# Four-branch mixer layers: the attention part rebuilt around four query tiles, one score tile and gates as filler

## Chip, cores and metric

One core of a Trainium2 chip. The metric is the device time of one launch in microseconds; the median of three runs stands for the kernel.

## Reference

Two layers over 256 context and 1024 latent tokens of width 1024. One input projection feeds four token mixers of width 256: A neighbourhood attention (clamped 8 x 16 window with a learned bias), B latent attention with a shared rotary key, C a bidirectional linear recurrence, D grouped-query attention. Each mixer's output is multiplied by the silu of a gate path; the branches are projected, gated and summed:

```
x = layer_norm(x) * (1 + scale) + shift
p = x @ w_in                                # mixers, silu gates z, merge gates m
y[i] = attend(q, k, v) or recurrence        # 4 heads of 64, softmax over context + latent keys
out = sum(sigmoid(m[i]) * ((y[i] * silu(z[i])) @ w_branch[i]) for i in range(4)) @ w_out
x = layer_norm(alpha * x + gate * out) * ln_g + ln_b
```

Context queries see context keys only, and the last layer needs no context output. All is float32.

## The kernel before

Tokens lie in 10 tiles of 128 (2 of context, 8 latent), all shared storage in 12 slots of 128 x 1280 (`slot`). A float32 operand is split into two parts, so each product is three matmuls (`mm_a` L271 to L273, `mm_b` L279 to L281; `hi_lo` L284, L285; `split_w` L233, L234; weights come by `load_w` L248). A scheduler turns the program into one instruction order per engine: a step that stands earlier in the program gets an engine first, a waiting instruction holds those behind it. Every load and store is issued by the sync engine's (SP) queue.

Each layer runs g_proj; then a weave of (m_proj, a_proj) with (lru, g_att), in proportion to expected numbers of steps; m_att; a_att; merge; last; outp. `g_att`, `m_att` and `a_att` loop over 4 heads. A head loads keys (high rows over low rows, `load_k` L641) and values (`load_v` L646), then `attend` takes two query tiles at a time: `load_q` (L632; L634 for the rotary rows of m) into one of two tiles, the scores of both, then puts off the value product of that unit by one unit (`defer`). A dense score tile (`dense_scores`, L618) goes bank by bank, 512 + 512 + 256 columns in three rotating banks, each read by VectorE with scale and maximum (L620); `softmax` joins the maxima (L587), takes the exponential on ScalarE (L592), the reciprocal of the sum (L596) and multiplies the row by it, on VectorE for the first tile (L599), on ScalarE for the second (L601). In `a_att` the bias rows be and bm are loaded (L804, L805), scaled on GpSimd, and added to the window's scores (L839 to L854). `values` transposes two key blocks of two query tiles into one bank (L552), splits it, and multiplies (L568, L569). `put_u` computes the silu gate of 128 output channels, multiplies, and writes u to memory.

While m_att and a_att run, `tick` emits steps of `gates`, which computes the merge gates of branch 0 (the one merged last) and writes them to memory (L885, L886). `merge` then takes branches 2, 3 and 1 (gates on PE, sigmoid L928, product and sum L934, L935), `last` takes branch 0 with the gates read back. The weave around the change:

```
weave(("", chain((f"m_proj{l}", m_steps()), (f"a_proj{l}", a_steps())), W_A),
      ("", chain((f"lru{l}", lru_steps()), (f"g_att{l}", g_att())), W_B + 4 * len(dense_units())))
```

## Time and profile before

| | us |
|---|---|
| median of 3 runs (lowest, highest) | 3183.25 (3182.18, 3184.07) |
| profiled execution, its own span | 3176.4 |
| PE busy | 2806.6 (88%) |
| VectorE busy | 1659.0 (52%) |
| ScalarE busy | 1382.4 (44%) |
| GpSimd busy | 208.7 (7%) |

The span runs from the first to the last instruction; the time around it is what a run has more. PE's mean granted clock is 0.946 of full speed. In the first layer, projections and lru end and g_att begins at about 300, m_att runs from 548 to 840, a_att to 1091, merge and last to 1570; the second layer's attention ends at 2709. A name such as `m_att__q` is a tile with the stage that was current when it was made. Busy time of PE at the lower clock counts in full, so a busy PE can still be slow.

### The profile page before, as it was taken

What the parts mean: (1) busy time and instruction counts of PE and PEld (TensorE: products, weight loads), DVE (VectorE), ACT (ScalarE), POOL (GpSimd) and SP (SyncE); (2) the same over time, 40 slices, a digit from 0 to 9 for tenths busy, and PEclk for the clock granted to TensorE, in tenths of its full rate; (3) what the DMA queues carried; (4) which work ended last, traced back from release to release, by engine and by line L of the source; (5) the groups of instructions that cost most, each with busy time, mean ns of one, the idle gap of its engine ahead of it and who ended that gap; (6) DMA issues with size and microseconds to landing.
All of it is one profiled execution on the core that took longest, in us unless ns stands there. A gap on an engine that the chain in (4) does not pass through costs nothing.

```text
span 3176.4 us, 40938 instructions
## 1 busy us (share of the span) xinstructions
PE 2806.6 (88%) x14798; PEld 2317.9 (73%) x14798; DVE 1659.0 (52%) x4049; ACT 1382.4 (44%) x2546; POOL 208.7 (7%) x273
## 2 busy tenths in 40 slices
PE   7999978778878999999999899878777688999998
PEld 4787767666767877777768787667666576888877
DVE  5666655555555512232377656556566456223356
ACT  4366655545555512121234456555555455222230
POOL 1200000000000000000042210000000100000031
PEclk9999989888988999999999999999898889999999
DMA  7233222211233322222353323222212222222142
GB/s 264 80 105 117 63 77 80 77 61 64 65 101 95 92 68 65 63 77 62 99 185 101 117 76 116 84 70 74 77 56 72 86 76 90 77 60 60 54 149 84
DMA packets 304563, 281.01 MB, mean 88 GB/s; under 512 B 23400, under 2 KB 249960, under 8 KB 304360
## 3 DMA queue, kind: packets, MB, share of 16 engines
q1 hardware_dynamic: 304360, 278.40, 28.4%
q8 instruction: 116, 1.90, 0.2%
q14 instruction: 87, 0.71, 0.1%
HBM read 207.67 MB, written 70.66 MB: 88 GB/s over the span
## 4 chain that ended last, share of the span: by engine, by line
PE 63%; DMA 17%; DVE 5%; ACT 4%; SPq 3%; issue 2%; POOL 2%; DVEq 0%; POOLq 0%; ACTq 0%
PE merge__mm L279 6%; PE merge__mm L280 6%; PE merge__mm L281 6%; PE m_att__s L618 3%; DMA m_att__q<-start__qkm 2%; PE a_att__mm L279 2%; PE a_att__mm L280 2%; PE a_att__mm L281 2%; DMA m_att__ks<-outp__qkm 2%; SPq L632 2%; PE m_att__t L552 2%; PE a_att__t L552 2%; PE merge__s L279 2%; PE merge__s L280 2%; PE merge__s L281 2%
## 5 line engine op out<-in xcount | busy, mean ns | idle before, releaser
L279 PE MATMUL merge__mm<-xh,merge__whi 128*128 128x512 f32 (+1 forms) x960 | 360.3, 375 | 0.0
L281 PE MATMUL merge__mm<-xh,merge__wlo 128*128 128x512 f32 (+1 forms) x960 | 354.8, 370 | 0.0
L280 PE MATMUL merge__mm<-xl,merge__whi 128*128 128x512 f32 (+1 forms) x960 | 354.8, 370 | 0.0
L279 PEld LDWEIGHTS merge__mm<-xh,merge__whi 128*128 128x128 f32 x960 | 181.5, 189 | 63.1 <-issue 21.6
L618 PE MATMUL m_att__s<-m_att__ks,m_att__q 128*128 128x512 f32 (+1 forms) x400 | 126.7, 387 | 96.9 <-DMA m_att__ks<-outp__qkm 47.4
L233 ACT CAST merge__whi<-merge__wraw 128x512 fp32r<-128x512 f32 x144 | 79.1, 551 | 290.4 <-PE merge__mm L280 243.9
L281 PEld LDWEIGHTS merge__mm<-xh,merge__wlo 128*128 128x128 f32 x960 | 181.6, 189 | 30.7
L280 PEld LDWEIGHTS merge__mm<-xl,merge__whi 128*128 128x128 f32 x960 | 181.7, 189 | 28.9
L928 ACT ACTIVATE merge__tmp<-merge__mm 128x512 f32<-128x512 f32 (+1 forms) x120 | 66.4, 553 | 312.0 <-PE merge__mm L281 311.2
L234 DVE TENSOR_TENSOR merge__wlo<-merge__wraw,merge__whi 128x512 fp32r<-128x512 f32 x144 | 86.4, 601 | 193.3 <-ACT merge__whi L233 187.9
L620 DVE TENSOR_SCALAR_CACHE_REDUCE m_att__p<-m_att__s 128x512 f32<-128x512 f32 (+1 forms) x200 | 113.7, 588 | 115.3 <-PE m_att__s L618 114.3
L284 ACT CAST m_att__ph<-m_att__t 128x512 fp32r<-128x512 f32 x164 | 94.5, 584 | 171.7 <-PE m_att__t L552 126.3
L934 DVE TENSOR_TENSOR merge__tmp<-merge__s,merge__tmp 128x512 f32<-128x512 f32 (+1 forms) x80 | 51.1, 638 | 220.6 <-PE merge__s L281 220.6
L618 PEld LDWEIGHTS m_att__s<-m_att__ks,m_att__q 128*128 128x128 f32 x400 | 76.3, 206 | 112.3 <-DMA m_att__ks<-outp__qkm 42.2
L285 DVE TENSOR_TENSOR g_att__pl<-g_att__t,g_att__ph 128x512 fp32r<-128x512 f32 x154 | 104.7, 688 | 84.8 <-ACT g_att__ph L284 70.9
L618 PE MATMUL g_att__s<-g_att__ks,g_att__q 128*128 128x512 f32 (+1 forms) x400 | 110.0, 381 | 38.6 <-DMA g_att__ks<-outp__qkg 19.6
L285 DVE TENSOR_TENSOR m_att__pl<-m_att__t,m_att__ph 128x512 fp32r<-128x512 f32 x164 | 111.1, 687 | 55.6 <-ACT m_att__ph L284 54.9
L620 DVE TENSOR_SCALAR_CACHE_REDUCE g_att__p<-g_att__s 128x512 f32<-128x512 f32 (+1 forms) x200 | 112.0, 586 | 42.2 <-PE g_att__s L618 41.3
L284 ACT CAST g_att__ph<-g_att__t 128x512 fp32r<-128x512 f32 x154 | 88.1, 583 | 100.6 <-PE g_att__t L552 52.4
L568 PE MATMUL g_att__pv<-g_att__ph,g_att__vs 128*128 128x256 f32 x308 | 98.1, 326 | 30.6 <-ACT g_att__ph L284 29.9
L279 PE MATMUL a_att__mm<-xh,a_att__whi 128*128 128x512 f32 (+1 forms) x304 | 119.0, 391 | 1.6 <-ACT a_att__tmp L885 1.6
L962 POOL TENSOR_TENSOR merge__acc<-merge__acc,last__spare 128x512 f32<-128x512 f32 (+1 forms) x40 | 55.9, 1421 | 939.0 <-DVE last__spare L961 938.8
(425 smaller groups left out, 7870.4 us busy)
## 6 DMA issues: line engine op xcount, KB each, us to landing
merge__wraw<-in_w_in_dram SPq DMA_DIRECT2D x96, 256.0 KB
mod__wm<-in_w_mod_dram SPq DMA_DIRECT2D x48, 256.0 KB
g_proj__wm<-in_w_mod_dram SPq DMA_DIRECT2D x16, 512.0 KB
a_att__wraw<-in_w_in_dram SPq DMA_DIRECT2D x32, 256.0 KB
last__wraw<-in_w_out_dram SPq DMA_DIRECT2D x32, 256.0 KB
merge__wraw<-in_w_branch_dram SPq DMA_DIRECT2D x48, 128.0 KB
g_att__q<-start__qkg SPq DMA_DIRECT2D x40, 128.0 KB
m_att__q<-start__qkm SPq DMA_DIRECT2D x40, 128.0 KB
```

The lines of the kernel that those rows point to most:

```text
L233: act.copy(hi[:, :n], raw[:, :n])
L234: dve.tensor_sub(lo[:, :n], raw[:, :n], hi[:, :n])
L279: pe.matmul(ps, wh, xh, start=first and k == 0, stop=False)
L280: pe.matmul(ps, wh, xl, start=False, stop=False)
L281: pe.matmul(ps, wl, xh, start=False, stop=last and k == nk - 1)
L284: act.copy(hi, src)
L285: dve.tensor_sub(lo, src, hi)
L552: pe.transpose(tb[:n, c:c + 128], pts[qi][:, col:col + n], ident)
L568: pe.matmul(pv[:, :nq], vt[:n, vb, :], ph[:n, w], start=first, stop=False)
L618: pe.matmul(s[:, :w], qs[:, j, qi * 128:(qi + 1) * 128], k[:, c0:c0 + w], start=j == 0, stop=j == len(ks) - 1)
L620: dve.tensor_scalar(pt[:, c0:c0 + w], s[:, :w], scale, None, ALU.mult, ALU.max, accum_out=mx[:, ns:ns + 1])
L928: act.activation(sgm[:, :g[1]], pm[:, :g[1]], AF.Sigmoid)
```

## The change

Twelve slots become thirteen. Attention works on units of four query tiles, with query loads and value products of 512 columns. The three score banks become one tile, `wide`, and the dense reduction is a single instruction of 1280 columns that gives the negated scores and the bias of the exponential. Rows of P stay unnormalised: the sums go to a column of `rcp`, and `put_u` multiplies the output by their reciprocals (GpSimd spreads them, PE transposes them). Silu uses tanh. `values` and `put_u` are generators in a queue; `pump` emits a share of the waiting steps behind each score tile. A list of 12 jobs covers the heads of g, m and a, and each head's keys and values are asked for when the head before it starts. Gates of two branches, 1 and 0, are computed as filler at one rate over all of the attention, and merge reads those of branch 1 from memory. Lru is woven with the projections, g_att no longer is. The core of the diff (removed lines only where they are short; where a whole function is replaced, the lines printed above give way):

```diff
-RATE_A = 3.0
+G_PRE = 2
...
-    sl = ctx.enter_context(tc.tile_pool(name="sl", bufs=12))
+    sl = ctx.enter_context(tc.tile_pool(name="sl", bufs=13))
...
-    ps_s = ctx.enter_context(tc.tile_pool(name="ps_s", bufs=3, space=PSUM))
+    ps_s = ctx.enter_context(tc.tile_pool(name="ps_s", bufs=1, space=PSUM))
...
     def sbank():
-        return ps_s.tile([128, 512], F32, tag="s", name=nm("s"))
+        turns[1] = (turns[1] + 1) % 3
+        return wide[:, 512 * turns[1]:512 * turns[1] + 512]
...
+    wide = ps_s.tile([128, 1536], F32, name="wide")
...
-        gate_d = dram([KC, 128, NT], F32, "gates")
+        gate_d = {i: dram([KC, 128, NT], F32, f"gates{i}") for i in M_ORDER[4 - G_PRE:]}
...
+        def put_u(i, c, y, rcp=None):
             w = load_chunk(w_in, C_Z + 256 * i + 128 * c)
+            if rcp is not None:
+                dve.reciprocal(rcp[:, :, q0t:], rcp[:, :, q0t:])
             for g in qgroups:
                 gs = slice(g[0], g[0] + g[1])
                 ps = mm()
-                mm_b(ps[:, :g[1]], w, xs_g(g))
+                xs = xs_g(g)
+                for k in range(0, KC, 2):
+                    mm_b(ps[:, :g[1]], w[k:k + 2], lambda j: xs(k + j), k == 0, k == KC - 2)
+                    if k < KC - 2:
+                        yield
                 s = tmp()
-                act.activation(s[:, :g[1]], ps[:, :g[1]], AF.Sigmoid)
-                dve.tensor_mul(s[:, :g[1]], ps[:, :g[1]], s[:, :g[1]])
-                dve.tensor_mul(y[:, gs], y[:, gs], s[:, :g[1]])
+                act.activation(s[:, :g[1]], ps[:, :g[1]], AF.Tanh, scale=0.5)
+                dve.scalar_tensor_tensor(s[:, :g[1]], s[:, :g[1]], 1.0, ps[:, :g[1]], ALU.add, ALU.mult)
+                if rcp is not None:
+                    tb = tbank()
+                    r = tmp()
+                    t0, n = g[0] // 128, g[1] // 128
+                    for j in range(n):
+                        pool.tensor_copy(r[:, j * 128:(j + 1) * 128].rearrange("p (h e) -> p h e", h=2),
+                                         rcp[:, :, t0 + j:t0 + j + 1].to_broadcast([128, 2, 64]))
+                    for j in range(n):
+                        pe.transpose(tb[:, j * 128:(j + 1) * 128], r[:, j * 128:(j + 1) * 128], ident)
+                    dve.tensor_mul(y[:, gs], y[:, gs], tb[:, :g[1]])
+                dve.scalar_tensor_tensor(y[:, gs], y[:, gs], 0.5, s[:, :g[1]], ALU.mult, ALU.mult)
+                yield
             sp.dma_start(u_d[i][c, :, QS], y[:, QS])
+            yield
+        PUT = 4 * len(qgroups) + 1
...
+                yield from put_u(2, c, hs[0])
...
+        queue, later = [], []
...
+        def pump(shares):
+            for _ in range(-(-sum(q[1] for q in queue) // shares)):
+                if queue:
+                    step()
...
+        def attend(h, y, rcp, units, loadq, scores, vt):
             o = 64 * (h % 2)
             for qts, blocks in units:
                 qs = loadq(qts[0] * 128, 128 * len(qts))
                 pts = []
                 for qi, qt in enumerate(qts):
+                    pts.append(scores(qs, qt, qi, rcp[:, h % 2, qt:qt + 1]))
                     tick()
+                    pump(len(qts) - qi)
+                    yield
+                queue.append([values(o, y, qts, blocks, pts, vt), len(blocks) + 1])
...
         def values(o, y, qts, blocks, pts, vt):
             nq = 128 * len(qts)
+            pv = ps_v.tile([128, 512], F32, tag="pv", name=nm("pv"))
             nb = len(blocks)
+            def turn(vb, q0, cols):
                 tb = tbank()
+                w = 128 * len(cols)
+                for i, col in enumerate(cols):
+                    pe.transpose(tb[:, i * 128:(i + 1) * 128], pts[q0 + i][:, col:col + 128], ident)
                 ph = tp.tile([128, 512], F32R, tag="ph", name=nm("ph"), bufs=2)
                 pl = tp.tile([128, 512], F32R, tag="pl", name=nm("pl"), bufs=2)
+                hi_lo(ph[:, :w], pl[:, :w], tb[:, :w])
+                return vb, slice(128 * q0, 128 * q0 + w), ph[:, :w], pl[:, :w]
+            def product(i, vb, qr, ph, pl):
+                pe.matmul(pv[:, qr], vt[:, vb, :], ph, start=i == 0, stop=False)
+                pe.matmul(pv[:, qr], vt[:, vb, :], pl, start=False, stop=i == nb - 1)
             st = None
+            for i, b in enumerate(blocks):
+                nx = turn(*b)
                 tick()
                 if st:
+                    product(i - 1, *st)
                 st = nx
+                yield
+            product(nb - 1, *st)
             lo = tmp()
             act.copy(lo[o:o + 64, :nq], pv[64 - o:128 - o, :nq])
             t0 = qts[0] * 128
             dve.tensor_add(y[o:o + 64, t0:t0 + nq], pv[o:o + 64, :nq], lo[o:o + 64, :nq])
+            yield
+        def softmax(pt, nb, spans, scale, total):
+            if len(spans) == 1:
+                (c0, c1), = spans
+                act.activation(pt[:, c0:c1], pt[:, c0:c1], AF.Exp, bias=nb, scale=scale, accum_out=total)
+                return
             sums = small(2, "sums")
             for j, (c0, c1) in enumerate(spans):
                 act.activation(pt[:, c0:c1], pt[:, c0:c1], AF.Exp, bias=nb, scale=scale, accum_out=sums[:, j:j + 1])
+            dve.tensor_add(total, sums[:, 0:1], sums[:, 1:2])
+        def new_y():
+            return slot(s="y"), lc.tile([128, 2, TT], F32, tag="rcp", name=nm("rcp"), bufs=3)
         def dense_units():
+            u = [((0, 1), [(b, 0, [b * 128] * 2) for b in range(CT)])] if need_ctx else []
+            full = [(b, 0, [b * 128] * 4) for b in range(TT)]
+            return u + [(tuple(range(CT + 4 * j, CT + 4 * j + 4)), full) for j in range(2)]
         def dense_scores(ks, scale):
+            def f(qs, qt, qi, total):
                 nk = CTX if qt < CT else NT
                 pt = slot(s="p")
+                nb = small(1, "nb")
                 for c0 in range(0, nk, 512):
                     w = min(512, nk - c0)
                     for j, k in enumerate(ks):
+                        pe.matmul(wide[:, c0:c0 + w], qs[:, j, qi * 128:(qi + 1) * 128], k[:, c0:c0 + w],
                                   start=j == 0, stop=j == len(ks) - 1)
+                dve.tensor_scalar(pt[:, :nk], wide[:, :nk], -scale, None, ALU.mult, ALU.min, accum_out=nb)
+                softmax(pt, nb, [(0, nk)], -1.0, total)
                 return pt
             return f
...
-            t = tp.tile([128, 3, 256], F32R, tag="q", name=nm("q"), bufs=2)
+            t = tp.tile([128, 3 if rope else 2, 512], F32R, tag="q", name=nm("q"), bufs=2)
...
+        def g_job(h):
+            def load():
                 if h % 2 == 0:
+                    g_kv[h // 2] = load_k(qk_g, 2, 64 * (h // 2)), load_v(v_g, h // 2)
+                return g_kv[h // 2]
+            def run(kv):
+                kd, vt = kv
+                if h % 2 == 0:
+                    g_y[h // 2] = new_y()
+                y, rcp = g_y[h // 2]
+                yield from attend(h, y, rcp, dense_units(), lambda t0, nq: load_q(qk_g, h // 2, 64 * (h % 2), t0, nq),
+                                  dense_scores([kd, kd], 0.125), vt)
                 if h % 2:
+                    queue.append([put_u(3, h // 2, y, rcp), PUT])
...
+                def scores(qs, qt, qi, total):
...
+                    w0 = 0 if rows == 8 else 224
+                    for c0, c1 in ((w0, 512), (512, w0 + n)):
+                        for i in range(2 if c1 > c0 else 0):
+                            pe.matmul(wide[:, c0:c1], qsl[i], kd[:, k0 + c0 - w0:k0 + c1 - w0], start=i == 0, stop=i == 1)
                     for i in range(2):
+                        pe.matmul(wide[:, 1024:1280], qsl[i], kd[:, :256], start=i == 0, stop=i == 1)
+                    dve.tensor_tensor_reduce(pt[:, :n], wide[:, w0:w0 + n], bias[:, bo:bo + n], 1.0, NEG,
                                              ALU.add, ALU.max, mx[:, 0:1])
+                    dve.tensor_scalar(pt[:, 640:896], wide[:, 1024:1280], 1.0, None, ALU.mult, ALU.max,
                                       accum_out=mx[:, 1:2])
+                    dve.tensor_scalar(nb, mx[:, 0:1], mx[:, 1:2], -0.125, ALU.max, ALU.mult)
+                    softmax(pt, nb, [(0, n), (640, 896)], 0.125, total)
                     return pt
                 units = []
...
+                for j0 in (0, 4):
+                    blocks = [(b, 0, [640 + b * 128] * 4) for b in range(CT)]
+                    lo = [NA_KEYROW[j] // 2 for j in range(j0, j0 + 4)]
+                    hi = [r + (NA_ROWS[j0 + i] + 1) // 2 for i, r in enumerate(lo)]
+                    for b in range(min(lo), max(hi)):
+                        js = [i for i in range(4) if lo[i] <= b < hi[i]]
+                        blocks.append((CT + b, js[0], [(b - lo[i]) * 128 for i in js]))
+                    units.append((tuple(range(CT + j0, CT + j0 + 4)), blocks))
+                yield from attend(h, y, rcp, units, loadq, scores, vt)
                 if h % 2:
+                    queue.append([put_u(0, h // 2, y, rcp), PUT])
+            return f"a_att{l}", load, run
...
+        def attention(jobs):
+            nx = jobs[0][1]()
+            yield
+            for i, (label, _, go) in enumerate(jobs):
+                cur = nx
+                phase[0] = label
+                if i + 1 < len(jobs):
+                    nx = jobs[i + 1][1]()
+                for _ in go(cur):
+                    yield
+                    phase[0] = label
         def gates():
+            for i in M_ORDER[4 - G_PRE:]:
+                for c in range(KC):
+                    w = load_chunk(w_in, C_GATE + i * D + c * 128)
...
+                        sp.dma_start(gate_d[i][c, :, gs], s[:, :g[1]])
+                        yield
+        att = attention([g_job(h) for h in range(4)] + [m_job(h) for h in range(4)] + [a_job(h) for h in range(4)])
         run(f"g_proj{l}", g_steps())
+        weave(("", chain((f"m_proj{l}", m_steps()), (f"a_proj{l}", a_steps())), W_A), (f"lru{l}", lru_steps(), W_B))
+        next(att)
+        ticks = 8 * (32 if need_ctx else 28) + 4 * (29 if need_ctx else 25)
+        fill.update(gen=gates(), rate=4 * KC * G_PRE * len(qgroups) / ticks, due=0.0)
+        for _ in att:
+            pass
+        flush()
...
-                    w = load_chunk(w_in, C_GATE + i * D + c * 128)
+                    w = None if i in gate_d else load_chunk(w_in, C_GATE + i * D + c * 128)
                     wb = load_chunk(a["w_branch"][l, i], c * 128, 2)
                     if bi == 0:
                         acc[c] = slot(s="acc")
                     for g in qgroups:
                         gs = slice(g[0], g[0] + g[1])
-                        pm = mm()
-                        mm_b(pm[:, :g[1]], w, xs_g(g))
                         sgm = tmp()
+                        if w is None:
+                            pm = sgm
+                            sp.dma_start(sgm[:, :g[1]], gate_d[i][c, :, gs])
+                        else:
+                            pm = mm()
+                            mm_b(pm[:, :g[1]], w, xs_g(g))
...
-    nc = bacc.Bacc("TRN2", target_bir_lowering=False, num_devices=1)
+    nc = bacc.Bacc("TRN2", target_bir_lowering=False, num_devices=1, dynamic_dma_scratch_size=1024)
```

How the order moves, at three places. First PE in m_att of the first layer, inside a head. Before, scores (`s`) of two tiles stand together, each bank its own tile:

```order
L618 MATMUL m_att__s_6503<-m_att__ks_6295,m_att__q_6486 128x256 x2
L618 MATMUL m_att__s_6503<-m_att__krs_5594,m_att__q_6486 128x256
L618 MATMUL m_att__s_6517<-m_att__ks_6295,m_att__q_6486 128x512 x2
L618 MATMUL m_att__s_6517<-m_att__krs_5594,m_att__q_6486 128x512
L618 MATMUL m_att__s_6522<-m_att__ks_6295,m_att__q_6486 128x512 x2
L618 MATMUL m_att__s_6522<-m_att__krs_5594,m_att__q_6486 128x512
```

and now the same place (t transposes, mm gate filler, pv value products):

```order
L638 MATMUL wide<-m_att__ks_5413,m_att__q_6365 128x256 x2
L638 MATMUL wide<-g_att__krs_4929,m_att__q_6365 128x256
L586 MATMUL m_att__t_6390<-ident,m_att__p_6347 128x128
L586 MATMUL m_att__t_6399<-ident,m_att__p_6347 128x128
L282 MATMUL m_att__mm_6441<-xh,m_att__whi_6302 128x512
L283 MATMUL m_att__mm_6441<-xl,m_att__whi_6302 128x512
L284 MATMUL m_att__mm_6441<-xh,m_att__wlo_6303 128x512
L593 MATMUL m_att__pv_6389<-m_att__ph_6395,m_att__vs_5415 128x512
L282 MATMUL m_att__mm_6441<-xh,m_att__whi_6308 128x512
L283 MATMUL m_att__mm_6441<-xl,m_att__whi_6308 128x512
L284 MATMUL m_att__mm_6441<-xh,m_att__wlo_6309 128x512
L638 MATMUL wide<-m_att__ks_5413,m_att__q_6365 128x512 x2
```

Between the last scores of a tile and the first of the next there are now two transposes and seven matmuls. Second, the sync engine's queue around the start of a head of a_att. Before (ks, vs, then the queries, then the bias):

```order
L641 DMA a_att__ks_9408<-start__qka_105 128x1x1280
L886 DMA start__gates_111<-a_att__tmp_9106 128x512
L646 DMA a_att__vs_9410<-start__va_108 128x10x128
L632 DMA a_att__q_9419<-start__qka_105 128x1x256 x2
L248 DMA a_att__wraw_10726<-in_w_in_dram 128x4x128
L804 DMA a_att__be_9412<-in_na_bias_dram 128x896
L805 DMA a_att__bm_9413<-in_na_bias_dram 128x576
```

and now:

```order
L650 DMA a_att__q_8401<-start__qka_106 128x1x256 x2
L928 DMA start__gates_8_113<-a_att__tmp_8328 128x512
L650 DMA a_att__q_8548<-start__qka_106 128x1x512
L659 DMA a_att__ks_8391<-start__qka_106 128x1x1280
L664 DMA a_att__vs_8393<-start__va_109 128x10x128
L841 DMA a_att__be_8395<-in_na_bias_dram 128x896
L842 DMA a_att__bm_8396<-in_na_bias_dram 128x576
L650 DMA a_att__q_8548<-start__qka_106 128x1x512
```

The keys and values in the second list are those of the next head, the bias and the queries those of the present one. Third, PE at the beginning of g_att in the first layer, now:

```order
L638 MATMUL wide<-lru__ks_3492,g_att__q_3532 128x256 x2
L586 MATMUL g_att__t_3546<-ident,g_att__p_3507 128x128
L586 MATMUL g_att__t_3569<-ident,g_att__p_3501 128x128
L586 MATMUL g_att__t_3569<-ident,g_att__p_3507 128x128
L593 MATMUL g_att__pv_3545<-g_att__ph_3549,lru__vs_3494 128x256
L638 MATMUL wide<-lru__ks_3492,g_att__q_3532 128x512 x4
```

Here the unit of context tiles is the only one whose values can be emitted, so little stands between two score tiles.

## Rows read from the trace of the kernel before

**Rows 1.** The page's first line and the head of its chain.

```profile
span 3176.4 us, 40938 instructions
...
PE 63%; DMA 17%; DVE 5%; ACT 4%; SPq 3%; issue 2%; POOL 2%; DVEq 0%; POOLq 0%; ACTq 0%
```

**Rows 2.** Busy time by stretch, projections to attention's end: each engine's us (instructions), clock, DMA share.

```profile
115.00:1091.00 976.00, 824.95 (x4783) 715.22 (x4782) 564.98 (x1595) 536.77 (x994) 37.91 (x59) 0.92 0.26 81
1806.00:2709.00 903.00, 742.08 (x4232) 633.54 (x4231) 516.52 (x1416) 493.29 (x882) 41.56 (x57) 0.91 0.26 80
```

**Rows 3.** The same view by stage: PE, PEld, DVE, ACT, POOL busy, then clock, DMA, GB/s.

```profile
115.00:300.00 185.00, 173.04 (x888) 148.07 (x887) 115.90 (x253) 102.51 (x223) 17.63 (x35) 0.98 0.33 101
300.00:548.00 248.00, 211.73 (x1332) 185.26 (x1331) 154.93 (x446) 148.19 (x244) 0.00 (x0) 0.93 0.24 75
548.00:840.00 292.00, 223.19 (x1292) 193.95 (x1291) 157.92 (x447) 148.64 (x243) 4.35 (x2) 0.87 0.23 72
840.00:1091.00 251.00, 216.98 (x1275) 187.95 (x1276) 136.22 (x451) 137.42 (x286) 15.93 (x22) 0.92 0.27 84
...
1806.00:1995.00 189.00, 171.05 (x883) 145.49 (x882) 112.36 (x225) 103.97 (x221) 21.53 (x33) 0.96 0.31 95
1995.00:2216.00 221.00, 183.87 (x1151) 159.81 (x1151) 138.50 (x389) 126.81 (x200) 0.00 (x0) 0.93 0.23 72
2216.00:2484.00 268.00, 201.51 (x1174) 174.14 (x1173) 147.56 (x401) 139.36 (x211) 4.11 (x2) 0.88 0.24 74
2484.00:2709.00 225.00, 185.66 (x1029) 154.09 (x1029) 118.10 (x403) 123.15 (x251) 15.91 (x22) 0.90 0.27 85
2709.00:3034.00 325.00, 324.95 (x1434) 268.79 (x1433) 103.66 (x163) 72.78 (x132) 0.00 (x0) 1.00 0.22 60
```

**Rows 4.** PE's waits in m_att, 548 to 840 and 2216 to 2484: us, times, longest.

```profile
PE m_att__s L618 <- DMA m_att__ks<-start__qkm: 33.3, 3, 12.1
PE m_att__s L618 <- DMA m_att__q<-start__qkm: 14.7, 10, 2.9
...
PE m_att__s L618 <- DMA m_att__ks<-outp__qkm: 41.1, 3, 14.4
PE a_att__s L839 <- DMA a_att__ks<-outp__qka: 11.0, 1, 11.0
```

**Rows 5.** PE's waits in a_att, 840 to 1091 and 2484 to 2709.

```profile
PE a_att__s L618 <- DMA a_att__q<-start__qka: 19.7, 4, 10.2
...
PE a_att__s L839 <- DMA a_att__q<-outp__qka: 37.2, 6, 14.6
```

**Rows 6.** The chain inside the first m_att, 548 to 840: start us, us, piece.

```profile
654.20 9.59 DMA m_att__q<-start__qkm
...
684.17 18.28 DMA m_att__q<-start__qkm
...
752.08 19.00 DMA m_att__ks<-start__qkm
```

**Rows 7.** SyncE's queue in m_att, 595 to 640: start us, us, instruction.

```profile
617.28 10.03 SPq L632 DMA_DIRECT2D m_att__q<-start__qkm  x1
```

**Rows 8.** PE's timeline, value products of 256 columns one behind the other.

```profile
648.02 0.28 PE L568 MATMUL m_att__pv<-m_att__ph,m_att__vs 128*128 128x256 f32 x1
648.14 0.28 PE L569 MATMUL m_att__pv<-m_att__pl,m_att__vs 128*128 128x256 f32 x1
```

**Rows 9.** VectorE's groups by shape, 548 to 840: busy us, mean ns, idle before.

```profile
L620 DVE TENSOR_SCALAR_CACHE_REDUCE m_att__p<-m_att__s 128x512 f32<-128x512 f32 x64 | 43.4, 685 | 20.5 <-PE m_att__s L618 20.2
L620 DVE TENSOR_SCALAR_CACHE_REDUCE m_att__p<-m_att__s 128x256 f32<-128x256 f32 x40 | 16.6, 418 | 36.3 <-PE m_att__s L618 36.0
```

**Rows 10.** VectorE's timeline: first and last instruction of lru's second half in the first layer.

```profile
244.21 0.94 DVE L459 TENSOR_SCALAR lru__lruc<-lru__lrux,lru__lrucols 128x1280 f32<-128x1280 f32 x1
...
303.84 0.68 DVE L422 TENSOR_TENSOR lru__lruo<-lru__lruo,lru__tmp 128x512 f32<-128x512 f32 x1
```

**Rows 11.** The page's groups: the multiplication of the second and third merged branch.

```profile
L934 DVE TENSOR_TENSOR merge__tmp<-merge__s,merge__tmp 128x512 f32<-128x512 f32 (+1 forms) x80 | 51.1, 638 | 220.6 <-PE merge__s L281 220.6
```

## Prediction before the result

> **What bounds the kernel now.** I read the page's head and chain first: TensorE (PE) works on 63% of the chain that ended last, transfers on 17%, every other engine on 5% or less [rows 1]. So the two things to price are PE's work and the places where PE stands still for a transfer. I took the program apart in stretches to find where it stands still. A stretch loses its length less PE's busy time multiplied by the granted clock: that counts idle time and time at the lower clock together. In the two merge stretches there is almost none (325.00 long, 324.95 busy, clock 1.00 [rows 3]). In the two stretches from the projections to the end of attention it is 976 − 824.95 × 0.92 = 217 and 903 − 742.08 × 0.91 = 228, together **445 us** [rows 2]; 312 of them are plain idle, so an idle microsecond costs 445 / 312 = 1.43 in all, because PE runs at the lower of its two clocks (1.2 instead of 2.4 GHz) for a while after a gap; the granted clock falls with the idle share, to 0.87 where a quarter is idle [rows 3].
>
> By stage [rows 3], the loss is 15 + 25 in the projections, 51 + 50 where g_att runs, 98 + 91 in m_att and 51 + 58 in a_att. What ends the idle time there is loads on the sync engine's queue: in m_att 33.3 + 14.7 + 41.1 + 11.0 = 100 of 135 idle us, in a_att 37.2 + 19.7 = 57 of 73 [rows 4, 5]. The chain through the first m_att says the same: a key load takes 19.00 us of it and a query load 18.28 [rows 6]. The queue's own timeline shows why a query load comes late: the one that follows the value load is issued only at 617.28, and that issue alone holds the queue 10.03 us, behind 1.25 MB of keys and values that were asked for when the head was about to start [rows 7].
>
> **The change, part by part.**
>
> *PE's work.* Value products go from 1776 matmuls of 256 columns to 944, mostly of 512. One of 256 starts 0.12 us after the other [rows 8], one of 512 takes 324.95 / 1434 = 0.227 us [rows 3]: 213 us become 199, **−14**. Transposes and scores stay within 2 us. The gates of branch 1 are moved, not removed: 384 matmuls of 512 and 192 of 256 in the first layer, 384 of 512 in the second, 110 + 87 = 197 us, leave the merge and enter the attention. The full-clock work of the two stretches was 1879 − 445 = 1434 and becomes 1434 + 197 − 14 = 1617, of which by the same prices (counts from the order) 437 are projections and lru, about 352 g, 448 m and 374 a.
>
> *Next head's keys and values.* They are issued ahead, at the head's start in the program (in the order about a query unit earlier than their use), and a head lasts some 60 to 73 us (251 and 292 us for four [rows 3]), so the waits of 33.3, 41.1 and 11.0 for keys should go. Queries come for four tiles, so in half as many waits. What is late next: the bias loads of a_att are still issued when its head begins, and now stand behind the *following* head's 1.25 MB, as does the second half of a query tile (second order excerpt). So I don't clear a_att: of its 109 us I keep 65, with 25 to 110 as the bounds.
>
> *g and m.* Without transfers m_att lost 35 idle us on 371 us of full-clock work [rows 3, 4], 9.5%; some of these are short query waits that I did not list. I take 8% of 352 + 448 = 800, **64** (bounds 2%, what the merge stands for, and 16%).
>
> *Single score tile.* Three banks in turn become one tile, read by one reduction. 512 columns take 685 ns and 256 take 418 [rows 9], so 1.04 ns a column, and 1280 take 1.49 us. PE may not write the next tile's scores until then. The first order excerpt shows two transposes, seven 512-column matmuls and so about 1.8 us of other work in between, so I take the wait as part of the 8%; uncovered it is the third rival. From Perfetto Trace Analysis, section Matmuls, the Trainium skill says: "Independent matmul groups should rotate through different PSUM banks so the ACT/DVE evacuation of one overlaps the next group's matmuls". By it the change gives back what rotation earned and the sum would be the third rival's; by the excerpt other work does that job.
>
> *Projections and lru.* g_att is no longer woven with the second half of lru. From convolution to output that chain took 244.21 to 303.84, 60 us [rows 10], with the cover of a_proj and g_att. Now the output gating is cut into 13 steps but the weave still counts 26 for lru, so some 20 steps come after the last projection. PE has lru's own gate matmuls and the first gate filler there. I take 12.5 us a layer uncovered (bounds 0 and half the chain, 30), plus 10 for the end of a_proj, plus today's 40: **75**.
>
> *Merge.* Its third branch now fetches gates instead of computing them: 24 steps in the first layer and 16 in the second, a full one 6 × 0.227 = 1.36 us on PE against a multiplication of 638 ns and an addition of about as much on VectorE [rows 11]: a tie at 1.3. With fetches through three buffers I take **+15** (0 to 40).
>
> *At nothing.* Normalisation of P leaves VectorE and ScalarE, which were busy 157.92 of 292 us in m_att on VectorE [rows 3]: neither is full, it only shortens the way from score to transpose. Half of the table loads (40 of 77 by the order) go from ScalarE. The new 108 broadcasts are on GpSimd, busy 37.91 of 976 us [rows 2]. If VectorE were late on a reduction, these would matter; that again is the third rival.
>
> *Sum* on the profiled execution: 3176.4 − 445 − 14 + 15 + (75 + 64 + 65) = 2936. The median of the runs, 3183.25, lies 6.9 above the span, so **2945 us** (rounded from 2943). My own range for this case is 2890 to 3020: all terms at their good ends would give about 2815, at their bad ends about 3110, and they will not all go one way.
>
> **Rivals.**
>
> *1. The key and query path is full, not late.* While m_att loads, the transfer engines are busy for 0.23 of the time, 72 GB/s [rows 3], and yet a key load takes 19 us of the chain and a query load 18 [rows 6]. If the same few transfer engines carry them, loading ahead orders the same bytes earlier and the heads keep their length. Then m stays 292 + 268 and a 251 + 225 [rows 3], g is at 380: 1416, with 437 + 75 in front 1928 instead of 1879. 3176.4 + 49 − 197 + 15 + 6.9 = **3050**. For it: query loads take 9.6 us on the chain even with no keys in front [rows 6]. Against: PE was idle for at most a third of a head. From DMA: Bandwidth & Descriptors, section Rules for kernel authors, the Trainium skill has it that an access whose outermost dimension is small keeps the whole DMA on that many engines, and the keys' and queries' outermost dimension here is two. By that rule 3050 would come out; no row of mine shows engines one by one. Chance 0.13.
>
> *2. All waits go.* The attention runs like the merge, the loss falls to about 110: **2850**. Against it: lru's tail and the bias loads. Chance 0.10.
>
> *3. Slower: PE waits for the one score tile.* Place: the first score matmul of each tile, behind the reduction. Price: 128 dense tiles × 1.6 us + 64 of a_att × 1.3 us = 288 us, × 1.43 for the clock = 412, so **3357**. It decides against the change from the point where 58% of it is uncovered ((3183 − 2945) / 412). For it: scores of two tiles stand back to back now, and in the first unit of g_att (third order excerpt) three transposes and a value product, 0.4 us, are all that stands between two tiles. Against: the first excerpt, which is the rule in the later units. Chance 0.07.
>
> *4. It doesn't do what it says.* Heads of m need the shared rope rows, two key, two value tiles, an output and up to 8 score rows: 14 slots, and there are 13. If the next keys get theirs only when the old head lets go, the 85 us of key waits stay, × 1.43 = 122, less what the 8% holds: **3050**. For it: the queue serves in order, so a load waiting for a slot also holds the queries. Against: the order excerpt puts that load behind the unit's queries. Chance 0.08.
>
> **How the numbers follow.** The forecast has 0.62, the rivals 0.13, 0.10, 0.07, 0.08. The range 2850 to 3060 takes in my own range, the middle of rivals 1 and 4 and the edge of rival 2; outside lie rival 3 and the halves beyond the others, about 0.2. A measurement here tells 0.2% (6 us) from none. Faster holds all but the third rival: 0.92; of that one a small part, 0.02, comes out even, and 0.06 slower.
>
> **What would show it.** Right: in the changed profile PE's waits for m_att keys vanish, the clock in m is above 0.95, the merge windows are 85 to 110 us shorter each, a_att still waits for bias or queries, and lru's end shows a dip. Wrong: if PE's largest wait is for VectorE at the score tile, rival 3; if for keys or queries with heads of about 70 us, rivals 1 or 4, told apart by whether the key load was *issued* a head ahead. The forecast fails outright if the loss in the two stretches stays above 330.

## Result: slower by 2.9%, and the profile after

The changed kernel takes 3280.61 us (median; 3272.3 to 3285.95) beside 3183.66 us for the kernel before in the same comparison: ratio **1.0294, 95% interval 1.0275 to 1.0313**. The forecast was 2945. Its profiled execution has a span of 3281.7 us, 346 more than the sum of the prediction without the time around the span (2936).

Busy time by stage of the changed kernel, columns as in [rows 3]: projections with lru; the gap before g_att; g, m, a; merge; then (last, outp and the next g_proj left out) the same stages of the second layer.

```profile
115.00:374.00 259.00, 242.78 (x1293) 204.91 (x1292) 116.00 (x254) 105.35 (x247) 16.92 (x36) 0.98 0.36 105
374.00:424.00 50.00, 15.19 (x69) 11.12 (x67) 14.50 (x11) 22.48 (x23) 0.00 (x0) 0.67 0.18 52
424.00:649.00 225.00, 196.82 (x1053) 162.02 (x1054) 126.81 (x221) 110.91 (x197) 2.72 (x10) 0.91 0.22 69
649.00:966.00 317.00, 258.42 (x1396) 214.42 (x1395) 135.25 (x217) 123.41 (x220) 5.30 (x20) 0.90 0.22 71
966.00:1236.00 270.00, 225.64 (x1278) 187.82 (x1277) 126.64 (x352) 116.72 (x289) 26.22 (x54) 0.92 0.28 89
1236.00:1626.00 390.00, 360.66 (x1698) 268.61 (x1697) 110.62 (x194) 77.42 (x151) 0.00 (x0) 0.96 0.30 83
...
1880.00:2137.00 257.00, 234.41 (x1245) 198.79 (x1243) 119.30 (x248) 109.86 (x246) 18.47 (x34) 0.95 0.33 98
2137.00:2173.00 36.00, 10.42 (x47) 8.02 (x46) 8.22 (x9) 12.85 (x15) 0.00 (x0) 0.71 0.23 72
2173.00:2364.00 191.00, 170.55 (x869) 138.68 (x870) 114.42 (x165) 99.52 (x161) 2.00 (x8) 0.93 0.25 76
2364.00:2610.00 246.00, 226.00 (x1145) 185.26 (x1144) 123.09 (x180) 110.78 (x182) 4.01 (x16) 0.95 0.25 80
2610.00:2872.00 262.00, 191.81 (x989) 157.07 (x988) 113.59 (x313) 105.77 (x254) 24.58 (x48) 0.87 0.25 77
2872.00:3141.00 269.00, 251.24 (x1061) 199.77 (x1059) 93.08 (x149) 64.03 (x117) 0.00 (x0) 0.97 0.27 76
```

By the same rule as in the prediction (length less busy time by clock), the stretches from the projections up to merge lose 21 + 40 + 46 + 84 + 62 in the first layer and 34 + 29 + 32 + 31 + 95 in the second, **475 us** where 204 were forecast and 445 were lost before. Merge, which lost next to nothing in the second layer, loses 44 + 25 = 69 where 15 were forecast. These two make 325 of the 346; last, outp and g_proj between the layers hold most of the rest (254 us beside 236). The loss of 475 is over the 330 at which the prediction called itself failed. PE's waits over the whole run (us, times, longest):

```profile
PE wide L872 <- DVE a_att__pa L877: 67.4, 4, 22.7
PE wide L872 <- DMA a_att__q<-start__qka: 41.4, 6, 18.2
PE m_att__t L440 <- POOL m_att__tmp L437: 33.6, 4, 12.8
PE wide L638 <- DMA lru__ks<-start__qkg: 32.5, 1, 32.5
PE wide L638 <- DMA lru__ks<-outp__qkg: 25.6, 1, 25.6
PE wide L282 <- DVE merge__tmp L980: 25.1, 30, 1.6
PE wide L638 <- DMA m_att__q<-start__qkm: 24.6, 3, 13.1
PE wide L638 <- DMA g_att__q<-start__qkg: 23.3, 2, 12.2
```

and VectorE's in the second a_att, which show what the first of these lines hides:

```profile
DVE a_att__pa L875 <- POOL a_att__be L843: 68.1, 4, 23.5
```

The 67.4 us is the bias: loaded late, scaled by GpSimd, then added by VectorE. Read by its name alone, the largest wait would have been the sign for rival 3, VectorE at the score tile. The key waits of m_att [rows 4] are gone as forecast. In their place stand the first head's keys (32.5 and 25.6), queries and bias. The sync engine's queue in the first head of g_att (start us, us) shows the mechanism:

```profile
456.68 0.50 SPq L650 DMA_DIRECT2D g_att__q<-start__qkg  x1
457.24 0.49 SPq L659 DMA_DIRECT2D g_att__ks<-start__qkg  x1
457.78 3.21 SPq L664 DMA_DIRECT2D g_att__vs<-start__vg  x1
461.04 13.66 SPq L650 DMA_DIRECT2D g_att__q<-start__qkg  x1
```

The next keys go out between the two halves of a query tile, and the second half holds the queue for 13.66 us behind them, as a query load did behind the present head's keys in [rows 7].

### The profile page after: what moved, and what is told of

It is laid out like the page before. It is cut to its first block, busy times and chain, and to the rows that moved or that the text cites. A ratio compares the mean times of both kernels' runs of the same rounds, so it can differ in the third digit from the quotient of the medians.

```text
span 3281.7 us, 38462 instructions
## 1 busy us (share of the span) xinstructions
PE 2821.1 (86%) x14042; PEld 2256.6 (69%) x14042; DVE 1548.2 (47%) x2955; ACT 1241.9 (38%) x2450; POOL 226.6 (7%) x381
## 5 line engine op out<-in xcount | busy, mean ns | idle before, releaser
L282 PE MATMUL merge__mm<-xh,merge__whi 128*128 128x512 f32 (+1 forms) x640 | 239.2, 374 | 0.0
L283 PE MATMUL merge__mm<-xl,merge__whi 128*128 128x512 f32 (+1 forms) x640 | 236.4, 369 | 0.0
L284 PE MATMUL merge__mm<-xh,merge__wlo 128*128 128x512 f32 (+1 forms) x640 | 236.1, 369 | 0.0
L640 DVE TENSOR_SCALAR_CACHE_REDUCE g_att__p<-wide 128x1280 f32<-128x1280 f32 (+1 forms) x72 | 98.6, 1370 | 127.3 <-PE wide L638 125.9
L288 DVE TENSOR_TENSOR m_att__pl<-m_att__t,m_att__ph 128x512 fp32r<-128x512 f32 (+1 forms) x168 | 111.3, 676 | 95.6 <-ACT m_att__ph L287 95.0
L640 DVE TENSOR_SCALAR_CACHE_REDUCE m_att__p<-wide 128x1280 f32<-128x1280 f32 (+1 forms) x72 | 98.7, 1371 | 73.5 <-PE wide L638 73.4
L282 PE MATMUL wide<-merge__uh,merge__whi 128*128 128x512 f32 (+1 forms) x240 | 97.2, 405 | 40.7 <-DVE merge__tmp L980 25.1
L282 PE MATMUL m_att__mm<-xh,m_att__whi 128*128 128x512 f32 (+1 forms) x304 | 122.6, 403 | 8.2 <-DVE m_att__tmp L431 8.2
L288 DVE TENSOR_TENSOR g_att__pl<-g_att__t,g_att__ph 128x512 fp32r<-128x512 f32 (+1 forms) x148 | 97.1, 673 | 67.7 <-ACT g_att__ph L287 67.4
L283 PE MATMUL a_att__mm<-xl,a_att__whi 128*128 128x512 f32 (+1 forms) x320 | 122.2, 382 | 0.0
L284 PE MATMUL a_att__mm<-xh,a_att__wlo 128*128 128x512 f32 (+1 forms) x320 | 121.3, 380 | 0.0
```

What stands on the lines that cost most here:

```text
L282: pe.matmul(ps, wh, xh, start=first and k == 0, stop=False)
L283: pe.matmul(ps, wh, xl, start=False, stop=False)
L284: pe.matmul(ps, wl, xh, start=False, stop=last and k == nk - 1)
L288: dve.tensor_sub(lo, src, hi)
L640: dve.tensor_scalar(pt[:, :nk], wide[:, :nk], -scale, None, ALU.mult, ALU.min, accum_out=nb)
```

## Experiments

Two theories. **P**: keys and queries use a narrow path (few of the 16 transfer engines), so that asking earlier only reorders a full queue. **D**: slices of the single score tile are not free one by one, so everything that used the three banks in turn loses the rotation. The rivals stand in the expectations. Medians are of four executions (of ten for a_3b). The ratios and their 95% intervals are to runs of the kernel before taken beside each version, whose median was 3178.05 to 3183.66, so differences of medians between versions are good to some 10 us.

**The path, in both kernels** (a_spread: changed kernel; b_spread: kernel before):

```diff
-            sp.dma_start(t.bitcast(F32), d[:, blk, r0:r0 + 64, :])
+            for i in range(2):
+                sp.dma_start(t.bitcast(F32)[64 * i:64 * i + 64, :], d[i, blk, r0:r0 + 64, :])
...
-                sp.dma_start(tf[:, i, :nq], d[i, blk, r0:r0 + 64, t0:t0 + nq][None].to_broadcast([2, 64, nq]))
+                for j in range(2):
+                    sp.dma_start(tf[64 * j:64 * j + 64, i, :nq], d[i, blk, r0:r0 + 64, t0:t0 + nq])
```

and the rotary rows of `load_q` likewise, in pieces of 32 rows.

> The changed kernel with each key load as two transfers of 64 rows and each query load as transfers of 64 (rotary: 32) rows, instead of one transfer whose outer dimension is 2; same bytes, same program place. Theory P (the path: keys and queries go over too few transfer engines, so loading ahead only moves the same queue): PE's waits for keys and queries, 152 us of idle, fall below 50, an idle microsecond costs 1.4, so about 3280 - 150 = 3130 us (3050 to 3180). Rival O (the order: loads are asked for too late or wait for slots behind the sync engine's queue): the waits stay, 3260 to 3300.

> The kernel before with the same two edits of the loads. Theory P: its 166 us of load waits in m_att and a_att mostly go, 3183 becomes about 2980 (2930 to 3050), so the kernel before, too, was held by the path and not by the late request. Rival O: a key load asked for at the head's start still has to come in before the first score; the waits shrink little, 3130 to 3190.

Measured: a_spread 2944.43 us, 0.9284 (0.925 to 0.9319); b_spread **2810.12 us, 0.8842 (0.8824 to 0.8859)**. Both are outside P's ranges: the gains are larger than P had said, by about 190 and 170 us. The loads of b_spread in m_att (KB each, median us to landing) and the m_att stages of b_spread and of a_spread:

```profile
m_att__q<-start__qkm SPq DMA_DIRECT2D x80, 64.0 KB, 2.2
...
m_att__ks<-start__qkm SPq DMA_DIRECT2D x8, 320.0 KB, 4.8
```

```profile
497.00:692.00 195.00, 194.79 (x1258) 171.97 (x1257) 150.65 (x433) 147.07 (x234) 0.00 (x0) 1.00 0.37 102
```

```profile
593.00:839.00 246.00, 246.00 (x1395) 206.90 (x1394) 134.21 (x217) 123.12 (x220) 5.29 (x20) 1.00 0.33 92
```

A query load of 64 KB lands in 2.2 us where one of 128 KB took 9.6 of the chain [rows 6]. PE runs without a gap at clock 1.00, and the 292 us of the first m_att [rows 3] are 195, with the keys still asked for at the head's start.

How many engines a load uses can be read from the DMA share, the busy part of the 16 engines, in a stretch with nothing else under way. First the kernel before while a key load and the query load behind it [rows 7] run, then b_spread while a key load runs (issued at 479.13, nothing behind it until 490.18; columns as in [rows 3]):

```profile
620.00:622.00 2.00, 0.00 (x0) 0.00 (x0) 1.02 (x2) 1.31 (x2) 0.00 (x0) 1.00 0.12 51
```

```profile
481.00:482.00 1.00, 1.00 (x11) 1.00 (x10) 1.00 (x6) 1.00 (x3) 0.00 (x0) 1.00 0.95 236
```

A share of 0.12 is two engines of 16, the size of the outer dimension, at 51 GB/s; spread, nearly all 16 work. Two transfers in place of one do not explain this: by the same count two engines each would make 0.25. P's path is shown. The change is now 134 us *behind*, although its m_att has no gap either: the rest is elsewhere. That its 2944 us meets the forecast of 2945 is luck: by the same rule it loses 82 us up to merge where 204 were forecast, 57 in the merges where 15 were, and its full-clock work up to merge is 1684 us where 1617 were.

**When the keys are asked for** (changed kernel, narrow loads):

```diff
-                if i + 1 < len(jobs):
-                    nx = jobs[i + 1][1]()
-                for _ in go(cur):
+                for _ in go(jobs[i][1]()):
```

> The changed kernel, but each head's keys and values are asked for when the head itself starts. Theory P with its part S (the next head's 1.25 MB stand in front of this head's second unit of queries): query waits (23 + 25 + 41 us in the first layer) fall, key waits of 10 to 30 us a head come back, and the two cancel to within 40 us: 3240 to 3320. Rival: loading ahead hides what it was meant to hide and its absence costs all key waits of the kernel before again, 85 us x 1.43 = 120 and more: above 3380.

Measured: 3393.99 us, 1.0684 (1.0652 to 1.0716). The rival holds: asking ahead is worth 113 us on the narrow path, so it did more than reorder the queue, against this part of P. PE's waits for queries are gone, but it waits for keys in every stage; in the first m_att:

```profile
PE wide L638 <- DMA m_att__ks<-start__qkm: 59.7, 4, 16.4
```

a_first moves `next(att)` ahead of the weave of projections and lru:

> The changed kernel with the first head's keys and values of g_att asked for ahead of the weave of the projections with lru instead of behind it. Theory F: the gaps at the start of g_att, which lose 40 and 29 us in the two layers, close: 3280 - 60 = 3220 (3205 to 3240). Rival: the two slots held through the weave make lru wait, or the queries come as late as the keys did: 3270 or more.

Measured: 3247.11 us, 1.023 (1.019 to 1.027). The first heads' key waits are gone, 34 us of the expected 60 come back; the wait for the queries of the first g_att grows from 23.3 to 31.6 us, and neither side's range holds.

**Keys alone spread** (the first edit of a_spread without the second):

> The changed kernel with the key loads alone spread, the query loads as they are. Theory S (the next head's keys stand in front of this head's queries on the same few engines): most of the gain of both edits is there, 3000 to 3060 us. Rival (the queries alone fill that path, 11 us for a unit of four tiles): less than a third of the gain, 3180 to 3270.

Measured: 3105.53 us, 0.9754 (0.974 to 0.9769): 175 of the 336 us, between the two ranges. The other half comes only when the queries are spread too; queries spread alone were not run.

**What the change still loses with spread loads.** a_spread_t takes merge and last off the score tile:

```diff
-                        pb = sbank()
+                        pb = tbank()
...
-        return (mm, sbank, mm, sbank, sbank)[turns[0] % 5]()
+        return (mm, tbank)[turns[0] % 2]()
```

> The changed kernel with the spread loads (2944 us), and with merge and last writing their products into the two transpose banks (last: into matmul and transpose banks) instead of slices of the one score tile. Theory D (a slice of the one tile isn't free until the slice written before it has been read, so the rotation over three banks is lost wherever slices are handed out): PE's waits of 27 us in merge and 13 us in last fall below 10 together, 2944 - 45 = 2900 us (2880 to 2915). Rival (the third branch waits for its gates to come back from memory): the waits move to another name and the time stays, 2930 to 2955.

Measured: 2934.61 us, 0.9221 (0.9205 to 0.9236): 10 us. PE's waits for `merge__tmp` fell from 27.4 to 15.3 us, those for `last__spare` from 13.3 to 11.0, not below 10 together. The time is in the rival's range, but two banks shared with transposes are no clean undoing of the tile.

a_spread_w replaces the plain weave by `chain((f"lru{l}", lru_steps()), (f"g_att{l}", g_att))` beside the projections:

> The changed kernel with the spread loads, and with the g heads woven with the projections behind lru, as in the kernel before; the gate filler runs over m and a alone, at a higher rate. Theory W (lru's chain lacks cover once g_att is taken out of the weave): about 45 us of what the projections lose more than in the kernel before with spread loads come back, 2900 us (2885 to 2920). Rival: that loss belongs to something else and g without filler loses as much again: 2935 to 2970.

Measured: 2938.84 us, 0.9231 (0.9216 to 0.9247): 6 us, in the rival's range; theory W fails here.

a_spread_g1 sets `G_PRE = 1`:

> The changed kernel with the spread loads, and gates of one branch instead of two as filler, so merge computes its third branch's gates again. Theory M (merge's third branch, with fetched gates and the one tile, is what merge loses): merge loses about 45 us less, attention no more than 10 more, 2905 us (2885 to 2925). Rival 3 of the prediction in a new form (attention lives on its filler): PE's waits for VectorE at the score tile grow by over 40 us, 2950 or more.

Measured: 2944.89 us, 0.9248 (0.9234 to 0.9262): no change; neither side is right. a_spread's own executions lie between 2933.91 and 2961.09, so the differences of 10, 6 and 0 us in these three runs (by the ratios 20, 17 and 11) are not told from each other.

**The one tile by itself.** b_spread_wide puts it into the kernel before and changes nothing else; a_spread_3b and a_3b take it out of the change, with the dense tile read bank by bank again, so that their price is net of what the single reduction saves. The edit of b_spread_wide:

```diff
-        return ps_s.tile([128, 512], F32, tag="s", name=nm("s"))
+        third[0] = (third[0] + 1) % 3
+        return wide[:, 512 * third[0]:512 * third[0] + 512]
```

> The kernel before with spread loads (2810 us), and one edit: its three rotating banks become slices of one tile, handed out in turn, as in the change. Nothing else moves. Theory D (a slice waits for the reader of the slice written before it): every user of the banks loses its rotation, 2920 us or more. Rival (only the same slice's reader is waited for): 2800 to 2825.

> The changed kernel with spread loads (2944 us), and three rotating banks in place of the one score tile everywhere; a dense tile is read bank by bank again, three reductions and a minimum over their results, and the window of a_att in two or three pieces. Theory D: the 130 us by which this kernel is behind the kernel before with spread loads come mostly from the one tile, outside attention: 2855 us (2825 to 2890). Rival (they come from put_u's many steps, the weave and the fetched gates): 2920 to 2955.

> The changed kernel with three rotating banks and its loads as they were. Theory D: the one tile's price is there whatever the loads do, 3281 - 100 = 3180 us (3150 to 3210), about even with the kernel before. Rival (the loads' waits hide the tile's): less than 40 us, 3240 or more.

| median us | three banks | one tile |
|---|---|---|
| before, narrow loads | 3183.66 | |
| before, spread loads | 2810.12 | 2965.6 |
| changed, narrow loads | 3187.47 | 3280.61 |
| changed, spread loads | 2859.68 | 2944.43 |

Ratios to the kernel before: b_spread_wide 0.9327 (0.9313 to 0.9341), a_spread_3b 0.8996 (0.8982 to 0.9009), a_3b 1.0027 (1.0017 to 1.0036). The tile costs 155 us in the kernel before, and 85 and 93 in the changed one with spread and narrow loads, so D's price is shown. It does not fall on every user of the banks, as D had it. The first m_att of b_spread_wide and of a_spread_3b (195 and 246 us above are b_spread and a_spread), then the first merge of b_spread, b_spread_wide, a_spread and a_spread_3b:

```profile
547.00:780.00 233.00, 214.76 (x1285) 177.65 (x1284) 161.29 (x435) 149.47 (x236) 0.00 (x0) 1.00 0.33 91
581.00:823.00 242.00, 241.97 (x1381) 204.65 (x1380) 143.70 (x382) 121.92 (x217) 5.29 (x20) 1.00 0.33 92
```

```profile
910.20:1394.00 483.80, 476.54 (x2335) 368.56 (x2335) 126.65 (x219) 92.39 (x177) 0.00 (x0) 0.99 0.25 72
998.90:1482.30 483.40, 476.34 (x2336) 368.38 (x2336) 127.13 (x219) 91.96 (x177) 0.00 (x0) 0.99 0.26 72
1055.00:1442.00 387.00, 357.98 (x1712) 267.41 (x1711) 110.36 (x193) 78.24 (x152) 0.00 (x0) 0.98 0.29 86
1043.00:1421.00 378.00, 357.42 (x1707) 266.99 (x1705) 110.73 (x197) 78.77 (x154) 0.00 (x0) 0.98 0.30 87
```

The kernel before pays in attention, 38 us in its first m_att, and nothing in merge, where in its program a branch's gate products stand between two slices. The changed kernel pays 4 us in the first m_att, where filler stands between them, and 9 in the first merge. The waits of b_spread_wide:

```profile
PE wide L621 <- DVE m_att__p L623: 13.5, 30, 0.8
...
PE wide L282 <- DVE last__spare L967: 9.6, 11, 1.8
PE wide L621 <- DVE g_att__p L623: 9.0, 17, 1.1
```

and a place in a_spread's merge (timeline, start us, us):

```profile
1401.96 0.28 PE L284 MATMUL wide<-merge__uh,merge__wlo 128*128 128x256 f32 x1
1402.28 0.42 DVE L983 TENSOR_TENSOR merge__tmp<-wide,merge__tmp 128x256 f32<-128x256 f32 x1 [0.96 <-PE wide L284]
...
1402.76 0.50 PE L282 MATMUL wide<-merge__uh,merge__whi 128*128 128x512 f32 x1 [0.52 <-DVE merge__tmp L983]
```

`sbank` hands out another slice for the next product, yet PE starts it 0.06 us after VectorE has read the *last* one (1402.28 + 0.42 = 1402.70). The wait is of the tile, not of the bytes: the order of the program, as built, holds the writer of one slice for the reader of another.

a_spread_3bw is a_spread_3b with the weave of a_spread_w:

> As the run before, with the g heads woven behind lru again. Theory D with W (the weave's cover is worth something once the banks rotate; with the one tile it came to nothing): 20 to 40 us less than with three banks alone, 2820 us (2790 to 2850). Rival: no difference beyond 10 us.

Measured: 2851.51 us, 0.897 (0.8957 to 0.8983): 8 us, so the rival holds: of W's 20 to 40 little is there.

**The last two.**

> The changed kernel with spread loads, three banks, g woven behind lru, and gates of one branch as filler (two: 2852 us). Theory G (what is left against the kernel before with spread loads, 2810 us, is mostly merge's third branch with fetched gates, 13 + 16 us of loss more than there): 2825 us (2812 to 2835). Rival (attention needs the second branch's gates as cover): 2845 or more.

Measured: 2839.61 us, 0.8924 (0.891 to 0.8938). This is between the two ranges. With all the rest mended, one filler branch in place of two is worth 12 us; 30 us against b_spread stay unexplained.

> The changed kernel with spread loads and three banks (2860 us), and each head's keys and values asked for at that head's own start. With narrow loads that cost 113 us. Theory P2 (the narrow path was the reason why a key load was late; over all engines it comes in 3 us or so): less than 20 us, 2855 to 2880. Rival (asking ahead is worth something by itself, as the load still stands behind the head's own queue): 2900 or more.

Measured: 2861.34 us, 0.8997 (0.8982 to 0.9012), 2 us from the version that asks ahead (2859.68). On the wide path asking ahead is worth nothing that can be measured; theory P2 holds, in the changed kernel with three banks.

## Why the prediction was wrong, by its own steps

- *What bounds the kernel* was read rightly (loads on the sync engine's queue, 1.43 us for each idle one), its cause was not. I took "late" for the cause; it was the path. b_spread gets 373 us out of the kernel before without one load being asked for earlier. I read the DMA share by stage only (0.23); in the short stretch shown above it is 0.12, and that row could have been read before.
- *Next head's keys and values*: the step that failed. It took the waits as a matter of when a load is asked for, on a path that carries 51 GB/s whenever that is. The waits priced (33.3, 41.1, 11.0) went, and a_noahead shows that they would have come back. But the transfers then stood in front of queries and bias: a_att lost 62 + 95 = 157 us where I kept 65 of 109 and bounded at 110. I named this place, and left it at a share of a_att.
- *The first head's keys* were not priced, a term left at nothing without a reason. After g_att left the weave nothing covers them: 40 + 29 us in two gaps; a_first gives 34 back.
- *g and m*: forecast 64, measured 46 + 84 + 32 + 31 = 193 on the narrow path. With spread loads a_spread's first m_att loses nothing, so on a wide path 64 would have been too much.
- *Single score tile*: the argument was right where I looked. In the attention of a_spread other work does hide it. But the same banks serve the projections, lru, merge, last and outp, where slices of one tile can follow each other with nothing between. Between the profiled runs of a_spread and a_spread_3b, 68 us apart, the attention has 7. I never asked who else takes from `sbank`. That is some 90 us, the whole distance from "even with before" (a_3b) to the result. The sentence of the Trainium skill cited there (Perfetto Trace Analysis, section Matmuls: groups should rotate through banks) agrees with b_spread_wide, where slices of one tile in place of banks cost 155 us.
- *Projections and lru*: forecast 75, measured 55 in the stretches without the gaps. *Merge*: forecast 15 (0 to 40), measured 69, of which some belongs to the tile; one branch of gates more or less as filler makes 12 us at the end of the series.
- *Rival 1* was the right mechanism at a chance of 0.13: its m stages, 560 us, came out at 317 + 246 = 563. That match is partly luck: one is 25 us longer than before, the other 22 shorter. Its time, 3050, was too low: it had no gaps before g_att (86 us long), g and a took 36 and 56 us more than it said, and the merges became 145 us shorter, not 182. The rule of the Trainium skill cited beside it (DMA: Bandwidth & Descriptors, section Rules for kernel authors: a small outer dimension keeps a transfer on at most as many engines) agrees with the trace: 0.12 of 16 engines with an outer dimension of two, 0.95 with rows of 64.
- *Rival 3* named a right suspect in the wrong place, and far too dear: it had 412 us, in attention; in the changed kernel the tile costs 85 to 93, nearly all outside it. *Rival 4* did not happen: m's keys were in time.
- GpSimd's broadcasts, costed at nothing, held PE for 33.6 us in m_att (the POOL line above). They are short themselves, but one waits for a gate store to leave its buffer:

```profile
849.85 1.00 POOL L437 COPY m_att__tmp<-m_att__rcp 128x128 f32<-128x128 f32 x4 [28.38 <-DMA start__gates<-m_att__tmp]
```

In a_spread, PE has no such wait in the first m_att and a_att; so this too depended on the crowded queue.

What stays open is the cause of the 30 us between a_spread_3bw_g1 and b_spread. In the profiled runs 26 of them lie in the projections with lru, from their first product to the first scores of g_att (378 us in the two layers, beside 352). b_spread, the kernel before with spread loads, is the fastest version run.

## What to carry to other kernels

When an engine waits for loads, ask first how wide a load is spread, then how early it is asked for: with the same bytes and the same moment, 64 rows in place of an outer dimension of 2 were worth 12%, and after that asking ahead was worth nothing. The sign here was a DMA share of 0.12 of 16 engines while PE stood still. Before joining buffers into one tile, list all who take from them, not only the loop for which it is done: a slice's writer may wait for the reader of another slice. A cover that is taken away (g_att beside the projections) must be priced with the first load that it hid.

## What the runs showed of the hardware

Loads whose outer dimension is 2 kept two of 16 transfer engines busy (share 0.12, 51 GB/s); with 64 rows outermost the share was 0.95 (236 GB/s). A load of 128 KB of the first kind took 9.6 us of the chain [rows 6]; one of 64 KB over 64 rows lands in 2.2 us, and keys of 320 KB in 4.8. One crowded load holds more than itself: an issue behind it held the sync engine's queue for 13.66 us, and bias (68.1 us of VectorE's waits) and gate stores (28.38 us of GpSimd's idle time) came late for other engines. Asking for these loads a head sooner was worth 113 us, and left PE waiting for the queries and the bias behind them.
